# A third pair of tiles for rounded weights, and a fourth Strassen step in the second output part of each FFN

## The chip, the cores and the metric

The kernel runs on one core of one Trainium2 chip. The core has five engines that run their own instruction streams and meet at semaphores: TensorE (PE in the profile; its weight loads are shown as PEld), VectorE (DVE), ScalarE (ACT), GpSimd (POOL) and SyncE (SP), which here issues most transfers. The metric is the time of one execution in microseconds, the median of several runs. The kernel before takes 2433.58 us, median of three runs (2432.37 to 2433.91).

## The reference

One layer of an encoder on 256 positions of width 2048, in float32. With LN for a layer norm and alpha = 2^(1/4):

```
h = LN(alpha*h + 0.5*FFN1(h))
h = LN(alpha*h + (sig(gA)*(A(h) WoA) + sig(gB)*(B(h) WoB)) W_out)   # two attentions, gated
h = LN(alpha*h + CrossAttn(h, LN(mem)))                              # 4 heads, 256 memory tokens
h = LN(alpha*h + 0.5*FFN2(h))
FFN(x): g, u = split(x @ w_in);  return (silu(g) * u) @ w_out        # w_in 2048 x 11008, w_out 5504 x 2048
```

Nearly all of the work is products of 256 rows of activations with weights that are read once each from memory.

## The kernel before

**Three products for one.** A float32 value is kept as two rounded parts, `hi` (the value cast to the type fp32r) and `lo` (what the cast left over, cast too). A product is then hi·hi + hi·lo + lo·hi, three matmuls, which `mm_pair` (L300 on) and `mm_sums` (L345 on) issue with the loops `for wi in range(2)` and `for xi in range(2 - wi)`. ACT casts a weight tile to `hi` in pieces of 1024 columns (L262), and DVE subtracts to get `lo` (L265); both lines are in `halves`.

**A step.** Weights come in tiles of 128 x 2048 (1 MB): two k-tiles of 128 rows by 1024 columns. Activations are the stationary side in blocks of 128 x 128, weights move 512 columns at a time. A plain step (`mm_pair`, matmuls at L309) has 2 k-tiles x 2 row halves x 2 column halves x 3 = 24 matmuls. They add into four PSUM banks, one for each row half and column half. The last step of an odd number of k-tiles has one k-tile and 12 matmuls.

**A Strassen step** (`mm_sums`, matmuls at L363) treats the same 2 x 2 x 2 blocks with seven products in place of eight, 7 x 3 = 21 matmuls. Three of the products go into three of the group's own banks, four into four further banks that all Strassen steps of the group share. For this DVE forms sums of the weights' blocks (`weight_sums`, L246 and L248: one addition of 128 x 1024 and two of 128 x 512), which are rounded into the tiles X2 and X3 (one set of them only), and sums of the activations' blocks (`sum_forms`, L319 and L323, rounded at L253 and L254). The raw tile's own part that is rounded is then 1536 columns wide and not 2048. After the last Strassen step of a group `shared` (L674 to L679) combines the four shared banks: ACT copies two of them, DVE makes four additions.

**Where the steps lie.** An FFN is computed in two parts of 24 and 19 k-tiles of its hidden width (`F_SPLIT`). For each part, groups of 512 hidden columns are computed from x (eight steps each, Strassen steps at 2, 4 and 6), multiplied, sent through a transposing transfer and split again (`hidden`), and then the part's output is added into `h`: 2048 columns in two halves of 1024. In the first part both halves run through `out_pair`, twelve steps with Strassen steps 3, 5, 7 and 9. In the second part the first half runs through `out_pair`, ten steps with Strassen steps 3, 5 and 7, the last step with one k-tile; the second half runs through `out_proj` (matmuls at L296) in order of its blocks, without Strassen steps. `SUMS_OUT` lists which step is a Strassen step, and in which tile its activations' forms live:

```
SUMS_OUT = ({3: ("X1", 0), 5: ("X1", 1), 7: ("X0", 0), 9: ("X0", 1)},
            {3: ("X1", 0), 5: ("X1", 1), 7: ("X0", 0)})
```

Forms in X1 are made during the hidden groups; those in X0 are woven into the output part, ahead of its item 4 + 2k for the slot k (`ffn`, the loop over `homes`). The last hidden group's turn, which its own part's steps 8 and 9 read, is woven in ahead of item 6. In `pair_group` the function `then` (the shared products are added to `h`, L626 or L628) comes behind the last Strassen step, and `finish` (the four own banks are added to `h`, L747 or L749, and a norm's statistics taken) behind the last step.

**What sets the order.** `run` walks a list of items (a function, with the weights that it needs) and emits the loading and rounding of weights ahead of the item that uses them:

```
return (nxt < need + 5 and (early(queue[nxt]) or n < 2)
        and held + live + slots(queue[nxt]) <= UNITS)
```

UNITS is 2, so at most two rounded units are emitted and not yet used, beside some that have homes elsewhere. The rounded tiles come from the pools `whi` and `wlo`, with UNITS buffers each, and the raw tiles from `wraw` with three; the transfer into a raw tile is issued by SP (L191). [...] 

**Short tiles.** The pool tag `w1` (128 x 256, 1 KB of a partition) holds running totals (`total`, L283 and L284) and the activations' forms that have no home; a set of forms takes four of them. [...]

Of the kernel before, what the change touches and what calls it, by code (L numbers as in the profile page):

```python
# [27 lines left out]
SUMS_IN = {2: ("X0", 0), 4: ("X0", 1), 6: None}  # L28
AT_FIRST = 4, 6
SUMS_OUT = ({3: ("X1", 0), 5: ("X1", 1), 7: ("X0", 0), 9: ("X0", 1)},  # L30
            {3: ("X1", 0), 5: ("X1", 1), 7: ("X0", 0)})
SUMS_YB = {4: ("T0", 0), 6: ("T0", 1), 2: None}
AT_YB = (2, 4, 6), (4, 6)
SUMS_XQ = {4: ("H5", 0), 6: ("H5", 1), 2: None}
# [5 lines left out]
SUM_HOME = ("X2", "X3"),  # L40
# [10 lines left out]
UNITS = 2  # L51
# [22 lines left out]
class Act:  # L74


    def __init__(self, blocks):
        self.blocks = blocks
# [21 lines left out]
class Kernel:  # L100
    def __init__(self, ctx, tc, t, out):
        self.tc, self.nc, self.t, self.out = tc, tc.nc, t, out

        def pool(name, bufs=1, **kw):
            return ctx.enter_context(tc.tile_pool(name=name, bufs=bufs, **kw))

        self.const = pool("const")
        self.wraw = pool("wraw", 3)
        self.whi = pool("whi", UNITS)
        self.wlo = pool("wlo", UNITS)  # L110
        self.blocks = pool("blocks")
        self.res = pool("res")
        self.work = pool("work", 4)
        self.small = pool("small", 4)
        self.ps_mm = pool("ps_mm", 4, space=PSUM)
        self.ps_at = pool("ps_at", 4, space=PSUM)
        self.items = []
        self.uid = 0
        self.chain = self.sent = self.last_hi = self.ln_act = None
        self.cut = self.early = False  # L120
# [13 lines left out]
        return self.work.tile(list(shape), dt, tag="w2", bufs=6, name=self.name("w2"))  # L134

    def w1(self, shape=(P, S), dt=F32):
        return self.work.tile(list(shape), dt, tag="w1", bufs=6, name=self.name("w1"))

    def sm(self, tag, n, dt=F32, bufs=None):
        return self.small.tile([P, n], dt, tag=tag, name=self.name(tag), **({"bufs": bufs} if bufs else {}))  # L140
# [410 lines left out]
    def ffn(self, tag, xT, st, first=None, steps=None, late=None, before=None, tags=None):  # L551


        t = self.t
        f0 = bank = 0
        turn = None
        fx = {}
        for half, nf in enumerate(F_SPLIT):
            hid, fh, homes = Act([]), {}, SUMS_OUT[half]
            end = half == len(F_SPLIT) - 1  # L560
            form = lambda c, fh=fh, homes=homes, hid=hid: self.forms_step(fh, homes, c, lambda: hid)
            for g in range(-(-nf // 4)):
                j, n = f0 // 4 + g, min(4, nf - 4 * g)
                qs, ps = {}, {}
                if j == 2 and first is not None:
                    self.add(self.load_rest)
                if j == 0 and first is not None:
                    main, (ps, qs, fx) = [], first
                    self.add(lambda qs=qs: self.shared(qs, 512), prio=SOON)
                elif j == 0 and before:  # L570
                    main = self.collect(self.first_group, tag, xT, before, ps, fx)
                else:
                    src = t[tag + "_w_in"][j] if n == 4 else t[tag + "_w_in_r"][0]
                    main = self.collect(self.pair_group, bank, src, n * P, KT, xT, SUMS_IN, fx, ps, qs, None, SUM_HOME + ("H5",))
                if turn and n < 4:
                    turn[5] = turn.pop(6)
                self.weave(main, turn or {}, prio=0)
                for c, (home, _) in homes.items():
                    if home == "X1" and c // 2 == g - 1:
                        self.add(form(c))  # L580
                hidden, turn = self.hidden(ps, bank, g, n, hid, qs)
                self.add(hidden, prio=SOON)
                if before and 2 <= j < 6:
                    self.add(lambda q=j - 2: self.gb_apply(2, self.h, (q,)), prio=LATE)
                if j == 0 and first is not None:
                    for c in set(SUMS_IN) - set(AT_FIRST):
                        self.add(self.forms_step(fx, SUMS_IN, c, xT, False))
                bank ^= 1
            if end and late:
                self.add(lambda: setattr(self, "cut", True))  # L590

            def out(hid=hid):
                x = lambda: hid
                src = [t[tag + "_w_out"][g, :, f0 * 1024:(f0 + nf) * 1024] for g in range(2)]
                self.out_pair(bank, src[0], 0, nf, x, homes, fh, half == 0, st if end else None,
                              SUM_HOME + ("H5",) if end else SUM_HOME)
                if end:
                    self.out_proj(tag + "_w_out_r", nf, x, False, st, steps, tags, 2, cut=tags is None)
                else:
                    self.out_pair(bank ^ 1, src[1], 1, nf, x, homes, fh, half == 0, None)  # L600
            main = self.collect(out)

            side = dict(turn)
            if end and late:
                side[len(main) - 6] = [late]
            for c, (home, k) in homes.items():
                if home == "X0":
                    side[4 + 2 * k] = side.get(4 + 2 * k, []) + [form(c)]
            if not end:
                for i in range(2):  # L610
                    side[len(main) - 3 + i] = [self.forms_step(fx, SUMS_IN, tuple(SUMS_IN)[i], xT)]
            self.weave(main, side, prio=0)
            turn = None
            f0 += nf

    def out_pair(self, bank, src, g, nk, x, at, fx, scale, st, sums_in=SUM_HOME):

        nc, h = self.nc, self.h
        ps, qs = {}, {}

        def shared():
            for (tt, a), s in qs["add"].items():
                c = (2 * g + a) * 512
                hs = h[tt][:, c:c + 512]
                if scale:
                    nc.vector.scalar_tensor_tensor(hs, hs, ALPHA, s, ALU.mult, ALU.add)  # L626
                else:
                    nc.vector.tensor_tensor(hs, hs, s, ALU.add)  # L628

        def finish():  # L630
            for tt in range(2):
                for a in range(2):
                    self.finish(tt, 2 * g + a, ps[tt, a], scale and not at, st)
        self.pair_group(bank, src, 512, nk, x, at, fx, ps, qs, shared, sums_in)
        self.add(finish)

    def group_tile(self, j):
# [2 lines left out]
    def group_tiles(self, j):  # L640
        return {(tt, g): self.group_tile(j) for tt in range(2) for g in range(2)}

    def pair_group(self, bank, src, n, nk, x, at, fx, ps, qs, then=None, sums_in=SUM_HOME):


        steps = -(-nk // 2)
        sums = [c for c in range(steps) if c in at]
        for c in range(steps):
            kts = range(2 * c, min(2 * c + 2, nk))
            ap = src[:, kts[0] * 2 * n:(kts[-1] + 1) * 2 * n]  # L650
            if c in at:
                def fn(w, c=c):
                    if c == sums[0]:
                        qs.update((a, self.group_tile(bank + 1)) for a in range(4))
                    self.mm_sums(ps, qs, w, n, x(), fx[c], 2 * c, c == sums[0], c == sums[-1])
                self.add(fn, Sums(ap, *sums_in))
                if c == sums[-1]:
                    self.add(lambda: self.shared(qs, n), prio=SOON)
                    if then:
                        self.add(then)  # L660
                continue

            def fn(w, c=c, kts=kts):
                if c == 0:
                    ps.update(self.group_tiles(bank))
                self.mm_pair(ps, w, n, x(), kts, c == 0, c == steps - 1)
            self.add(fn, ap)

    def shared(self, qs, n):
# [1101 lines left out]
```

## Time and profile before

| what | value |
|---|---|
| median of three runs | 2433.58 us (2432.37 to 2433.91) |
| the profiled execution, span from first to last instruction | 2432.9 us |
| what the median has over that span | 0.7 us |
| PE busy | 2423.0 us, 11286 matmuls |
| DVE busy | 2121.1 us, 2423 instructions |
| ACT busy | 1551.3 us, 2017 instructions |
| transfers | 516.20 MB, 212 GB/s on average |
| granted clock of PE | 1.000 |

The profile tells of the profiled execution only its span, so the span stands for its time. Busy time counts an engine's instructions; matmuls are pipelined, so a matmul's own duration is longer than its distance from the next. The list of waits gives for each engine and line whom it waited for, the time in total, the number of waits and the longest. The chain of waits follows the work that ended last, in order of time, as start, duration and what ran. A timeline row has start, duration, engine, line, operation, output and inputs, and in brackets the idle time before it and what ended that.

### The profile page before, as it was taken

Reading aid. Unit: us, or ns where it says so; the run is one execution under the profiler, and the core shown is the slowest. Engines: PE = TensorE matmul, PEld = TensorE weight load, DVE = VectorE, ACT = ScalarE, POOL = GpSimd, SP = SyncE. Lnnn points to the kernel's source line nnn. Section 1 sums busy time; section 2 is a strip of 40 time slices with the busy share of each in tenths; the row PEclk is TensorE's granted clock in tenths of the full one; section 3 lists DMA queues with packets and bytes.
Section 4 is the critical chain, followed back from the end, with each engine's and each line's share of the span. In section 5 each row is a group of like instructions: output and inputs, shape, how many; then the busy total and the mean of one; then the engine's idle time right before and its main releaser. Section 6 shows DMA issues by size and latency. Waiting matters only on the chain.

```text
span 2432.9 us, 29701 instructions
## 1 busy us (share of the span) xinstructions
PE 2423.0 (100%) x11286; PEld 2022.5 (83%) x11286; DVE 2121.1 (87%) x2423; ACT 1551.3 (64%) x2017; POOL 36.1 (1%) x81
## 2 busy tenths in 40 slices
PE   9999999999999999999999999999999999999999
PEld 8888888889888888888888888888888888888887
DVE  8999989899878898789788889979879999888997
ACT  6676745666555557878565687765666675556762
POOL 0000000000000001000000000000000000000000
PEclk9999999999999999999999999999999999999999
DMA  7766656666645657776577577655556666666665
GB/s 268 252 214 213 208 199 221 212 199 222 225 172 209 208 209 248 230 209 175 184 249 251 167 236 218 219 184 189 190 199 214 229 221 210 216 208 205 201 223 182
DMA packets 176414, 516.20 MB, mean 212 GB/s; under 512 B 111728, under 2 KB 112496, under 8 KB 121104
## 3 DMA queue, kind: packets, MB, share of 16 engines
q1 hardware_dynamic: 170816, 495.83, 61.2%
q0 software_dynamic: 4592, 17.30, 2.2%
q8 instruction: 88, 1.44, 0.2%
q10 hardware_dynamic: 864, 1.18, 0.1%
q14 instruction: 54, 0.44, 0.1%
HBM read 485.30 MB, written 2.10 MB: 200 GB/s over the span
## 4 chain that ended last, share of the span: by engine, by line
PE 90%; DVE 4%; ACT 3%; DMA 1%; issue 1%; SPq 0%; DVEq 0%; ACTq 0%
PE at L309 24%; PE mm L309 23%; PE mm L296 11%; PE at L363 10%; PE mm L363 10%; PE mm L275 5%; PE mm L277 2%; DVE lo L265 2%; ACT hi L262 1%; PE at L1028 1%; DMA raw<-w_xq 0%; PE at L1499 0%; PE at L1082 0%; PE at L275 0%; DMA raw<-w_o_b 0%
## 5 line engine op out<-in xcount | busy, mean ns | idle before, releaser
L262 ACT CAST hi<-raw 128x1024 fp32r<-128x1024 f32 (+1 forms) x852 | 805.3, 982 | 454.2 <-PE at L309 155.0
L265 DVE TENSOR_TENSOR lo<-raw,hi 128x2048 fp32r<-128x2048 f32 (+1 forms) x427 | 902.3, 2114 | 139.3 <-ACT hi L262 133.4
L309 PE MATMUL mm<-hi,T 128*128 128x512 f32 (+1 forms) x1328 | 311.1, 384 | 1.3 <-DVE v L397 1.3
L309 PEld LDWEIGHTS mm<-hi,T 128*128 128x128 f32 x1328 | 247.3, 188 | 48.5 <-DVE v L397 1.8
L309 PE MATMUL at<-hi,T 128*128 128x512 f32 x1152 | 275.5, 389 | 0.0
L262 ACT CAST X<-H 128x1024 fp32r<-128x1024 f32 (+1 forms) x166 | 170.6, 1034 | 162.0 <-DVE H L246 128.1
L309 PEld LDWEIGHTS at<-hi,T 128*128 128x128 f32 x1152 | 216.2, 188 | 45.1
L265 DVE TENSOR_TENSOR X<-H,X 128x2048 fp32r<-128x2048 f32 (+1 forms) x83 | 186.7, 2250 | 68.6 <-ACT X L262 68.6
L309 PE MATMUL mm<-lo,T 128*128 128x512 f32 (+1 forms) x664 | 160.4, 382 | 0.0
L309 PEld LDWEIGHTS mm<-lo,T 128*128 128x128 f32 x664 | 123.7, 188 | 22.8
L309 PE MATMUL at<-lo,T 128*128 128x512 f32 x576 | 142.4, 389 | 0.0
L309 PE MATMUL at<-hi,H 128*128 128x512 f32 x560 | 133.7, 389 | 0.0
L309 PEld LDWEIGHTS at<-lo,T 128*128 128x128 f32 x576 | 108.1, 188 | 22.5
L309 PEld LDWEIGHTS at<-hi,H 128*128 128x128 f32 x560 | 104.9, 188 | 21.6
L309 PE MATMUL mm<-hi,H 128*128 128x512 f32 x480 | 115.5, 391 | 0.3 <-DVE w L679 0.3
L248 DVE TENSOR_TENSOR H<-H,raw 128x512 f32<-128x512 f32 (+1 forms) x166 | 112.2, 676 | 2.2
L309 PEld LDWEIGHTS mm<-hi,H 128*128 128x128 f32 x480 | 89.5, 188 | 19.3 <-DVE w L679 0.8
L246 DVE TENSOR_TENSOR H<-raw 128x1024 f32<-128x1024 f32 (+1 forms) x83 | 99.4, 1198 | 0.9 <-DMA raw<-w_gate 0.8
L363 PE MATMUL mm<-X,X 128*128 128x512 f32 x342 | 91.1, 392 | 0.0
L262 ACT CAST X<-raw 128x1024 fp32r<-128x1024 f32 (+1 forms) x54 | 55.4, 1036 | 48.7 <-DVE raw L248 38.7
L363 PE MATMUL at<-X,X 128*128 128x512 f32 (+1 forms) x315 | 82.5, 386 | 0.9 <-DVE X L265 0.5
L849 ACT COPY w<-w 128x1024 uint16<-128x1024 uint16 (+1 forms) x60 | 75.8, 1276 | 0.6 <-DMA w<-w 0.5
(373 smaller groups left out, 4123.1 us busy)
## 6 DMA issues: line engine op xcount, KB each, us to landing
raw<-ffn_w_in SPq DMA_DIRECT2D x150, 1024.0 KB, 4.8
raw<-ffn_w_out SPq DMA_DIRECT2D x66, 1024.0 KB, 4.8
raw<-w_gate SPq DMA_DIRECT2D x32, 1024.0 KB, 4.8
raw<-ffn_w_out_r SPq DMA_DIRECT2D x16, 1024.0 KB, 4.9
raw<-w_qk SPq DMA_DIRECT2D x16, 1024.0 KB, 5.5
raw<-w_o_b SPq DMA_DIRECT2D x16, 1024.0 KB, 4.8
raw<-w_out SPq DMA_DIRECT2D x16, 1024.0 KB, 5.2
raw<-w_xk SPq DMA_DIRECT2D x16, 1024.0 KB, 5.3
```

Of the source, the lines that this page charges most:

```text
L246: self.nc.vector.tensor_tensor(two[0], two[1], raw[:, :m].unsqueeze(1).to_broadcast([P, 2, m]), ALU.add)
L248: self.nc.vector.tensor_tensor(t[:, a * m:a * m + m], t[:, b * m:b * m + m], raw[:, a * m:a * m + m], ALU.add)
L262: self.last_hi = self.nc.scalar.copy(hi[:, c:d], src[:, c:d])
L265: self.last_lo = self.nc.vector.tensor_tensor(lo[:, :n], src, hi[:, :n].bitcast(F32), ALU.subtract)
L275: self.nc.tensor.matmul(ps, hi[j], x.both(kt), start=(j == 0), stop=False)
L277: self.last_mm = self.nc.tensor.matmul(ps[:, :S], lo[j], x.at(0, kt), start=False, stop=(j == n - 1))
L296: self.last_mm = self.nc.tensor.matmul(ps, x.at(xi, kt)[:, tt * P:(tt + 1) * P], w[wi][:, j * 512 + c:j * 512 + c + m], start=(start and j ...
L309: self.last_mm = self.nc.tensor.matmul(ps[tt, g][:, :n], x.at(xi, kt)[:, tt * P:(tt + 1) * P], w[wi][:, c:c + n], start=first and j + wi + ...
L363: self.last_mm = self.nc.tensor.matmul(bank[:, :m], a[xi], v[wi][:, c * m:(c + 1) * m], start=own and first and wi + xi == 0, stop=own and ...
L849: self.nc.scalar.copy(self.words(u, n).rearrange("p (c k) -> p k c", k=2), self.words(s, n).rearrange("p (k c) -> p k c", k=2))
L1028: nc.tensor.matmul(ps[:, c0:c0 + nk], q[:, tt * P:(tt + 1) * P], k[:, :nk], start=(j == 0), stop=(j == len(parts) - 1))
```

## The change

`whi` and `wlo` get UNITS + 1 = 3 buffers each; UNITS, and with it the order in which loads are emitted, stays 2. That takes 16 KB more of each partition. The tag `w1` gets five buffers in place of six, and the scratch for GpSimd's descriptors is set to 1024 bytes, where the library's default stood before. In the second output part of each FFN step 1 of the first half becomes a Strassen step, its forms in the second slot of X0, and the steps run in the order 0, 2, 3, 4, 5, 6, 7, 8, 1, 9. `out_pair` and `pair_group` take that order as an argument; first and last step, which open and close the sums in PSUM, go by the place in the order.

```diff
 SUMS_OUT = ({3: ("X1", 0), 5: ("X1", 1), 7: ("X0", 0), 9: ("X0", 1)},
-            {3: ("X1", 0), 5: ("X1", 1), 7: ("X0", 0)})
+            {3: ("X1", 0), 5: ("X1", 1), 7: ("X0", 0), 1: ("X0", 1)})
+ORDER_END = (0, 2, 3, 4, 5, 6, 7, 8, 1, 9)
...
-        self.whi = pool("whi", UNITS)
-        self.wlo = pool("wlo", UNITS)
+        self.whi = pool("whi", UNITS + 1)
+        self.wlo = pool("wlo", UNITS + 1)
...
-        return self.work.tile(list(shape), dt, tag="w1", bufs=6, name=self.name("w1"))
+        return self.work.tile(list(shape), dt, tag="w1", bufs=5, name=self.name("w1"))
...
-                              SUM_HOME + ("H5",) if end else SUM_HOME)
+                              SUM_HOME + ("H5",) if end else SUM_HOME, ORDER_END if end else None)
...
-        steps = -(-nk // 2)
-        sums = [c for c in range(steps) if c in at]
-        for c in range(steps):
+        order = range(-(-nk // 2)) if order is None else order
+        sums = [c for c in order if c in at]
+        for i, c in enumerate(order):
...
-            def fn(w, c=c, kts=kts):
-                if c == 0:
+            def fn(w, i=i, kts=kts):
+                if i == 0:
                     ps.update(self.group_tiles(bank))
-                self.mm_pair(ps, w, n, x(), kts, c == 0, c == steps - 1)
+                self.mm_pair(ps, w, n, x(), kts, i == 0, i == len(order) - 1)
...
-    nc = bacc.Bacc("TRN2", target_bir_lowering=False, num_devices=1)
+    nc = bacc.Bacc("TRN2", target_bir_lowering=False, num_devices=1, dynamic_dma_scratch_size=1024)
```

The arrangement of `w_out` in memory follows from `SUMS_OUT` by itself: the host swaps the two column halves of a Strassen step's k-tiles, now for step 1 too.

More of the change, by code (lines that the diff above doesn't have):

```diff
@@ L614, in ffn, with out_pair @@
             f0 += nf
-    def out_pair(self, bank, src, g, nk, x, at, fx, scale, st, sums_in=SUM_HOME):
+    def out_pair(self, bank, src, g, nk, x, at, fx, scale, st, sums_in=SUM_HOME, order=None):
         nc, h = self.nc, self.h
@@ L633, in finish @@
                     self.finish(tt, 2 * g + a, ps[tt, a], scale and not at, st)
-        self.pair_group(bank, src, 512, nk, x, at, fx, ps, qs, shared, sums_in)
+        self.pair_group(bank, src, 512, nk, x, at, fx, ps, qs, shared, sums_in, order)
         self.add(finish)
@@ L641, in group_tiles, with pair_group @@
         return {(tt, g): self.group_tile(j) for tt in range(2) for g in range(2)}
-    def pair_group(self, bank, src, n, nk, x, at, fx, ps, qs, then=None, sums_in=SUM_HOME):
-        steps = -(-nk // 2)
-        sums = [c for c in range(steps) if c in at]
-        for c in range(steps):
+    def pair_group(self, bank, src, n, nk, x, at, fx, ps, qs, then=None, sums_in=SUM_HOME, order=None):
+        order = range(-(-nk // 2)) if order is None else order
+        sums = [c for c in order if c in at]
+        for i, c in enumerate(order):
             kts = range(2 * c, min(2 * c + 2, nk))
```

## The prediction

> **What bounds the kernel now.** I read the page's engine shares first, then TensorE's waits, then the chain of waits around one part of the change, then how busy VectorE is there.
>
> ```profile
> span 2432.9 us, 29701 instructions
> PE 2423.0 (100%) x11286; PEld 2022.5 (83%) x11286; DVE 2121.1 (87%) x2423; ACT 1551.3 (64%) x2017; POOL 36.1 (1%) x81
> ```
>
> TensorE (PE) works nearly the whole span, VectorE (DVE) 87% of it. What PE waits for is short enough to be listed whole:
>
> ```profile
> PE mm L309 <- DVE v L397: 1.3, 1, 1.3
> PE at L490 <- DVE w L467: 1.1, 1, 1.1
> PE at L418 <- issue: 0.7, 1, 0.7
> PE at L363 <- DVE X L265: 0.5, 1, 0.5
> PE at L363 <- ACT X L262: 0.4, 2, 0.2
> PE mm L363 <- DVE T L254: 0.4, 1, 0.4
> PE mm L309 <- DVE w L679: 0.3, 1, 0.3
> PE at L1082 <- ACT H L849: 0.2, 1, 0.2
> PE mm L275 <- ACT hi L262: 0.2, 1, 0.2
> ```
>
> Sum 5.1 us, of which 1.1 (L490) is the start, which the change doesn't touch; 4.0 us is all the waiting that it could take away. Only 0.2 us of that is named on a weight's rounding `hi`. So the time is matmuls in a row, and less time comes from fewer matmuls. The chain of waits over the second output part of the first FFN shows what one costs:
>
> ```profile
> 580.48 16.36 PE at L309 x72
> 596.84 0.91 PE at L363 x4
> ...
> 601.37 0.23 PE at L363
> 601.60 5.44 PE at L309 x24
> ...
> 617.24 0.91 PE at L363 x4
> ...
> 622.00 8.16 PE at L309 x36
> 630.16 49.64 PE mm L296 x219
> ```
>
> Steps 0 to 2 are 72 matmuls in 16.36 us, 0.227 us each. A plain step of two k-tiles is 24 of them (5.44 us); a Strassen step (L363) takes from 596.84 to 601.60, 4.76 us, which is 21. Steps 8 and 9, after the third Strassen step, are the 36 from 622.00; at 630.16 the second half of the columns begins.
>
> **Part 1, the fourth Strassen pair.** In each FFN step 1 becomes a Strassen step and moves between steps 8 and 9. PE loses 24 − 21 = 3 matmuls, 3 × 0.227 = 0.68 us; two FFNs, −1.36 us. [...]
>
> What DVE does for one Strassen step, from its timeline in the same place:
>
> ```profile
> 593.77 0.68 DVE L319 TENSOR_TENSOR w<-H 128x512 f32<-128x512 f32 x1
> ...
> 594.98 0.48 DVE L323 TENSOR_TENSOR w<-w 128x128 f32<-128x128 f32 x2
> 595.38 0.61 DVE L323 TENSOR_TENSOR w<-w,w 128x128 f32<-128x128 f32 x2
> ...
> 604.96 0.68 DVE L254 TENSOR_TENSOR X<-w,X 128x512 fp32r<-128x512 f32 x1
> ...
> 611.78 1.22 DVE L246 TENSOR_TENSOR H<-raw 128x1024 f32<-128x1024 f32 x1
> 612.91 1.75 DVE L265 TENSOR_TENSOR lo<-raw,hi 128x1536 fp32r<-128x1536 f32 x1
> 614.58 0.68 DVE L248 TENSOR_TENSOR H<-H,raw 128x512 f32<-128x512 f32 x1
> ...
> 617.50 2.29 DVE L265 TENSOR_TENSOR X<-H,X 128x2048 fp32r<-128x2048 f32 x1 [0.70 <-ACT X L262]
> 619.71 2.29 DVE L265 TENSOR_TENSOR lo<-raw,hi 128x2048 fp32r<-128x2048 f32 x1
> ...
> 622.51 1.22 DVE L265 TENSOR_TENSOR lo<-raw,hi 128x1024 fp32r<-128x1024 f32 x1
> ...
> 626.04 1.89 DVE L628 TENSOR_TENSOR h<-h,w 128x512 f32<-128x512 f32 x3
> ```
>
> Added: the weights' sums, 1.22 + 2 × 0.68 = 2.58; the low half of those sums (L265, `X`), 2.29; the activations' forms, 0.68 + 0.48 + 0.61 + 0.68 = 2.45. Saved: 1536 columns rounded in place of 2048, 2.29 − 1.75 = 0.54. Net 2.58 + 2.29 + 2.45 − 0.54 = +6.8 us of DVE in each FFN. ScalarE (ACT) gets two more casts of the sums and one of the forms, less half a cast: by the mean of 1034 ns,
>
> ```profile
> L262 ACT CAST X<-H 128x1024 fp32r<-128x1024 f32 (+1 forms) x166 | 170.6, 1034 | 162.0 <-DVE H L246 128.1
> ```
>
> 2 × 1.03 + 0.5 − 0.5 = about 2.1 us. No transfer is added: the same 1 MB of weights is loaded, as another kind of step. Does it fit? The stretches:
>
> ```profile
> 500.00:530.00 30.00, 30.00 (x134) 24.82 (x133) 29.42 (x33) 21.65 (x27) 0.00 (x0) 1.00 0.72 211
> 580.00:630.00 50.00, 50.00 (x223) 41.42 (x221) 46.41 (x49) 30.91 (x37) 0.00 (x0) 1.00 0.65 225
> 630.00:650.00 20.00, 20.00 (x90) 16.57 (x89) 13.44 (x13) 7.51 (x9) 0.00 (x0) 1.00 0.60 200
> 251.00:303.00 52.00, 52.00 (x232) 43.04 (x230) 50.31 (x53) 36.05 (x43) 0.00 (x0) 1.00 0.61 198
> 2321.00:2371.00 50.00, 50.00 (x223) 41.50 (x222) 46.41 (x49) 30.59 (x37) 0.00 (x0) 1.00 0.66 227
> ```
>
> (Columns: stretch, its length, busy time of PE, PEld, DVE, ACT, POOL, clock, DMA share, GB/s.) The part takes 50 us with DVE busy 46.41 of it, alike in both FFNs. It becomes 49.3 us with 46.41 + 6.8 = 53.2 us of DVE work: 3.9 too much if nothing can wait. ACT, 30.91 + 2.1 of 49.3, is no bound. But after the rounding for step 8 (done at 622.0) PE needs only the 1.22 us of step 9 before 630; the other 6.8 us of those 8.0 (combining the shared products, adding them to `h`, the first rounding of the next half) can slip past 630, where DVE is busy only 13.44 of 20 us. What PE needs by the end of the new Strassen step, at 630.16 − 0.68 − 2.72 = 626.8 (step 9 is 12 matmuls), is then 53.2 − 6.8 − 1.2 = 45.2 us of work in 46.8 us, 97%. DVE ran at 98% from 500 to 530, and at 97% from 251 to 303 where Strassen and plain steps alternate in the same way, and PE lost nothing in either. I take the added wait as 0, by that nearest row; the bounds are 0 and 3.9 us in each FFN. A gain below 0 is excluded, since PE does not wait in these stretches now.
>
> Three shifts of order go with it. Step 3 comes one plain step earlier, after two and not three; that is also the order in the input groups (Strassen steps 2, 4 and 6), which fill 500 to 530. The turning of the last hidden group, woven in at the seventh item, stands one plain step nearer to step 8, which reads it; PE has one Strassen step (4.76 us) between, and its DVE work is two short subtractions. And the four banks of shared products are read out with only step 9 (2.72 us) before the next half wants two of them; those two need ACT copies alone, and ACT is a third idle here. All three are costed at nothing; if the cover is gone, what is late is PE, by the parts of a us that its waits above show (up to 1.3), and this lies inside the 3.9.
>
> **Part 2, the third pair.** Loading is still limited by UNITS = 2, so a rounding stands where it stood in each engine's order; only its wait for a free tile ends one unit earlier. These are the waits of ACT that it shortens, the three largest groups:
>
> ```profile
> ACT hi L262 <- PE at L309: 155.0, 77, 5.0
> ACT hi L262 <- PE mm L309: 119.8, 68, 5.4
> ACT hi L262 <- PE mm L296: 42.3, 13, 4.3
> ```
>
> 317 us of ACT's idle time, none of it PE's: what ends later is that PE is in work while ACT waits. The roundings behind them come up to 5.4 us sooner, and the raw tiles come free sooner for the next loads. In PE's list only the 0.2 us at L275 names `hi`; I take a gain of 0, with 4.0 us (the whole list without the start) as the most. On the other side, this pool changes when the planner believes each rounding ready, everywhere, and the planner picks each engine's order from that; bulk roundings of 2.29 us may land ahead of a short chain that PE waits for. The row nearest is the 1.3 us at L397 (such a chain in a layer norm). One more of that size at each of the five changes of stage (FFN to mixer, attention to its output, to cross attention, out of it, and into the last norm) is 6.5 us, the other bound.
>
> **Part 3, what pays for it.** Five short tiles `w1` in place of six: forms without a home hold four of them, so one is left for running totals, but these live in other stages. PE's list names no wait on a total (L283, L284); 0, at most another 0.2 us like L1082's. The scratch for GpSimd's transfers is set to 1024 bytes, where it was left at its default. Should that make an issue wait for the one before it to land, the price is this landing time:
>
> ```profile
> w<-gb POOLq DMA_DIRECT2D x24, 256.0 KB, 4.2
> ```
>
> Four stand close together once, so 3 × 4.2 = 12.6 us late at worst, for a multiply by the norm's gain; behind that in DVE's order stand roundings, and behind those PE. POOL is busy 1% of the span, and the pairs elsewhere stand apart, so I take 0. [...]
>
> **The sum.** −1.36 + 0 + 0 + 0. The profiled execution's span is 2432.9 us; the three runs have a median of 2433.58, so 0.7 us lies around the span. 2433.58 − 1.36 = **2432.2 us**.
>
> **The rivals.** *DVE becomes the bound* (the slower side). The sum of the weights for step 1 and its forms come on top of the turn and the plain rounding for step 8, and X2 and X3 exist once, so the third pair cannot start them early. If nothing slips past 630, PE waits 3.9 us in each FFN: 2433.58 − 1.36 + 7.8 = 2440.0. It decides once DVE's lateness passes 0.68 us in each FFN, and shows as slower from (4.9 + 1.36)/2 = 3.1. Against it: the two stretches at 97 and 98%. For it: here DVE already stands waiting for casts in between (0.70 at 617.50). *The third pair clears PE's waits*: 2433.58 − 1.36 − 4.0 = 2428.2. Against it: eight of nine rows name something else than a weight's rounding. *The planner's new order costs*: 2433.58 − 1.36 + 6.5 = 2438.7; for it, that every stage is planned anew, against it, that roundings done sooner are out of the way later. *Nothing happens, because PE was not the bound*: 2433.6. [...] The even 0.227 us per matmul across every quoted piece speaks against it.
>
> **How the numbers follow.** Forecast 0.60 (2430.5 to 2434.5, with up to 1.1 us of late DVE in each FFN, or half of PE's waits gone); DVE late 0.18; new order costs 0.11; waits cleared 0.06; nothing 0.05. About 0.2% (4.9 us) is what a measurement of this kernel can tell from no change, so faster begins at 2428.7 and slower at 2438.4. The gain of part 1 alone is far inside. Faster needs nearly all of the waits cleared: 0.06. Slower needs the far half of the two bad rivals: 0.13. The range leaves out these far ends: 2428.8 to 2438.2.
>
> **What would show it.** Right: 11280 matmuls; between the first out step and the next half, 49.3 us in both FFNs; no wait of PE over 1 us on `X` or `lo` at L363 there; ACT's waits for PE at `hi` cut from 317 us to a small part; POOL's loads land as before. Wrong: PE waits on DVE `X` in the new step (DVE the bound), new waits over 1 us at L418, L1028 or L275 (new order), or PE's list shrunk to under 2 us (waits cleared).

## The result and the profile after

The changed kernel takes 2463.43 us (median of four executions, 2463.03 to 2465.23) against 2433.43 beside it: ratio 1.0124, interval 1.011 to 1.0139. It is **slower by 30 us**. The forecast was 2432.2, and the range ended at 2438.2. One execution of one kernel below, the one with DVE and ACT chained, took 5366 us, for a reason not known; its other nine lie from 2428.87 to 2431.46.

The page of the changed kernel:

```profile
span 2461.8 us, 29644 instructions
PE 2429.0 (99%) x11280; PEld 2025.5 (82%) x11280; DVE 2132.7 (87%) x2443; ACT 1550.1 (63%) x2023; POOL 36.1 (1%) x81
```

The six matmuls are gone, DVE has 20 instructions and 11.6 us more, and yet the span is 28.9 us longer. With the 1.36 us of matmuls saved, 30.3 us are to be found. The first rows of its list of PE's waits (engine, line and whom it waited for: total us, times, longest):

```profile
PE mm L276 <- DVE w L285: 7.7, 2, 7.3
PE mm L310 <- DVE w L680: 6.7, 7, 2.9
PE at L364 <- ACT X L263: 3.8, 5, 1.2
PE at L310 <- DVE w L680: 2.5, 3, 1.1
PE mm L310 <- DVE w L285: 1.8, 1, 1.8
```

All twelve rows of that list sum to 28.1 us, 27.0 without the 1.1 of the start, where before had 4.0: 23.0 of the 30.3. (Line numbers after are one higher from L31 on: L680 is L679 of before.) L680 is the last step of the combination of the shared products, L285 the sum of two halves of a bank; both read PSUM, and PE waits at L276 and L310 for the bank that they free (7.3 and 2.9 us at the longest). Two such waits, in the timeline of the changed kernel (start, us, engine, line, operation, and in brackets the idle time before and what ended it):

```profile
1056.41 2.29 DVE L266 TENSOR_TENSOR lo<-raw,hi 128x2048 fp32r<-128x2048 f32 x1 [1.50 <-ACT hi L263]
1058.62 1.01 DVE L1056 SCALAR_TENSOR_TENSOR w<-at,X 128x384 f32<-128x384 f32 x2
...
1060.66 0.41 DVE L285 TENSOR_TENSOR w<-w,mm 128x256 f32<-128x256 f32 x1
...
1061.12 2.07 PE L276 MATMUL mm<-X,hi 128*128 128x512 f32 x4 [7.31 <-DVE w L285]
...
1518.20 0.69 DVE L678 TENSOR_TENSOR w<-w,w 128x512 f32<-128x512 f32 x1
1518.93 2.29 DVE L266 TENSOR_TENSOR lo<-raw,hi 128x2048 fp32r<-128x2048 f32 x1
...
1521.14 0.68 DVE L679 TENSOR_TENSOR w<-w,mm 128x512 f32<-128x512 f32 x1
1521.74 0.68 DVE L680 TENSOR_TENSOR w<-w,mm 128x512 f32<-128x512 f32 x1
...
1522.47 2.08 PE L310 MATMUL mm<-hi,H 128*128 128x512 f32 x4 [2.94 <-DVE w L680]
```

In the first, a bulk rounding of 2.29 us, which itself waited for its cast on ACT, stands ahead of the total of 1060.66, with 2.0 us of softmax work (from L1056 on) between them. In the issue order of the third pair alone, which has this same wait, the rounding and its two casts are the only instructions of DVE and ACT that stand ahead of this total and stood behind it in the kernel before; the softmax work stood ahead of it there too. In the second, a bulk rounding of 2.29 us stands between L678 and L679, in the middle of a chain for which PE waits. The second place in the kernel before:

```profile
1503.81 0.69 DVE L677 TENSOR_TENSOR w<-w,w 128x512 f32<-128x512 f32 x1
1504.53 0.69 DVE L678 TENSOR_TENSOR w<-w,mm 128x512 f32<-128x512 f32 x1
1505.14 0.68 DVE L679 TENSOR_TENSOR w<-w,mm 128x512 f32<-128x512 f32 x1
...
1505.87 1.42 PE L309 MATMUL mm<-hi,H 128*128 128x512 f32 x5 [0.33 <-DVE w L679]
```

There the chain runs in a row, and PE waits 0.33 us. Three of the longer waits in the changed kernel are followed by matmuls at a lower granted clock. Its stretches (length, busy time of PE, PEld, DVE, ACT, POOL, granted clock, DMA share, GB/s):

```profile
1061.00:1065.00 4.00, 3.88 (x11) 3.30 (x12) 2.72 (x12) 4.00 (x12) 0.00 (x0) 0.50 0.06 14
1519.00:1526.00 7.00, 4.06 (x12) 2.92 (x11) 7.00 (x9) 4.51 (x6) 0.00 (x0) 0.76 0.11 21
1619.00:1626.00 7.00, 5.17 (x17) 3.90 (x16) 5.15 (x7) 3.36 (x7) 0.00 (x0) 0.76 0.78 313
```

A clock of 0.50 over 4.0 us, and twice 0.76 over 7.0 us, where the trace has 0.50 for 3.41 us and 1.00 around it: (1 − 0.76) × 2 × 7 = 3.4 us. That is 10.8 us in which the matmuls of 512 columns start 0.427 us apart, where 0.227 is usual: by estimate 10.8 × (1 − 0.227/0.427) = 5.1 us lost. With 23.0 that makes 28.1 of 30.3; the rest lies in delays too short for the list. Matched by the number of the matmul, the kernel is 7.2 us behind at 636 us (the first FFN), 6.9 at 1050, 16.9 at 1094 (attention), 13.7 at 1468, 24.2 at 1718 (cross attention), 24.4 at 2215 and 30.3 at 2439 (the second FFN). The loss comes in four places, and most of it not where the fourth Strassen step was put.

The waits of ACT for PE at `hi`, which the prediction wanted cut to a small part, are still there, and two groups that wait for transfers have grown, from 3.7 us (`ffn_w_in`) and 14.1 us (`ffn_w_out`) before:

```profile
ACT hi L263 <- PE at L310: 108.9, 56, 3.8
ACT hi L263 <- DMA raw<-ffn_w_in: 92.2, 37, 4.8
ACT hi L263 <- PE mm L310: 83.5, 37, 3.7
ACT hi L263 <- DMA raw<-ffn_w_out: 44.2, 26, 4.2
```

### The profile page after: what moved, and what is told of

It reads as the page before. It is cut to its first block, busy times and chain, and to the rows that moved or that the text cites. A ratio compares the mean times of both kernels' runs of the same rounds, so it can differ in the third digit from the quotient of the medians.

```text
span 2461.8 us, 29644 instructions
## 1 busy us (share of the span) xinstructions
PE 2429.0 (99%) x11280; PEld 2025.5 (82%) x11280; DVE 2132.7 (87%) x2443; ACT 1550.1 (63%) x2023; POOL 36.1 (1%) x81
## 4 chain that ended last, share of the span: by engine, by line
PE 71%; DVE 11%; ACT 8%; DMA 5%; issue 4%; SPq 0%; DVEq 0%; ACTq 0%
PE mm L310 19%; PE at L310 19%; PE mm L297 9%; PE mm L364 8%; PE at L364 8%; DVE lo L266 4%; ACT hi L263 3%; PE mm L276 3%; DMA raw<-ffn_w_in 2%; PE mm L278 2%; PE at L1029 1%; ACT w L850 1%; ACT X L263 1%; DVE H L247 1%; DMA raw<-w_xv 1%
## 5 line engine op out<-in xcount | busy, mean ns | idle before, releaser
L263 ACT CAST hi<-raw 128x1024 fp32r<-128x1024 f32 (+1 forms) x852 | 802.9, 981 | 535.0 <-PE at L310 108.9
L310 PE MATMUL mm<-hi,T 128*128 128x512 f32 (+1 forms) x1328 | 310.7, 384 | 4.0 <-DVE w L680 3.5
L310 PEld LDWEIGHTS mm<-hi,T 128*128 128x128 f32 x1328 | 247.2, 188 | 52.6 <-DVE w L680 5.6
L310 PE MATMUL at<-hi,T 128*128 128x512 f32 x1152 | 275.2, 390 | 1.4 <-DVE w L680 1.4
L310 PEld LDWEIGHTS at<-hi,T 128*128 128x128 f32 x1152 | 215.8, 188 | 47.8 <-DVE w L680 3.1
L310 PE MATMUL mm<-lo,T 128*128 128x512 f32 (+1 forms) x664 | 159.7, 382 | 0.0
L310 PE MATMUL at<-lo,T 128*128 128x512 f32 x576 | 142.6, 389 | 0.0
L310 PEld LDWEIGHTS mm<-lo,T 128*128 128x128 f32 x664 | 123.6, 188 | 22.8
L310 PE MATMUL at<-hi,H 128*128 128x512 f32 x528 | 126.9, 390 | 1.1 <-DVE w L680 1.1
L310 PEld LDWEIGHTS at<-lo,T 128*128 128x128 f32 x576 | 108.1, 188 | 22.5
L310 PE MATMUL mm<-hi,H 128*128 128x512 f32 x480 | 118.8, 399 | 5.0 <-DVE w L680 3.2
L310 PEld LDWEIGHTS at<-hi,H 128*128 128x128 f32 x528 | 98.8, 188 | 22.2 <-DVE w L680 1.5
L310 PEld LDWEIGHTS mm<-hi,H 128*128 128x128 f32 x480 | 91.5, 192 | 25.6 <-DVE w L680 4.5
L364 PEld LDWEIGHTS mm<-X,X 128*128 128x128 f32 x360 | 67.0, 188 | 16.9 <-ACT X L263 1.8
```

Source lines behind the costliest of these rows:

```text
L263: self.last_hi = self.nc.scalar.copy(hi[:, c:d], src[:, c:d])
L310: self.last_mm = self.nc.tensor.matmul(ps[tt, g][:, :n], x.at(xi, kt)[:, tt * P:(tt + 1) * P], w[wi][:, c:c + n], start=first and j + wi + ...
L364: self.last_mm = self.nc.tensor.matmul(bank[:, :m], a[xi], v[wi][:, c * m:(c + 1) * m], start=own and first and wi + xi == 0, stop=own and ...
```

## The experiments

The kernel before, timed beside them, had a median of 2433.2, 2433.16 and 2433.32 us in the three groups of runs.

### The two parts alone

The third pair with what pays for it, and no fourth step:

```diff
-        self.whi = pool("whi", UNITS)
-        self.wlo = pool("wlo", UNITS)
+        self.whi = pool("whi", UNITS + 1)
+        self.wlo = pool("wlo", UNITS + 1)
...
-        return self.work.tile(list(shape), dt, tag="w1", bufs=6, name=self.name("w1"))
+        return self.work.tile(list(shape), dt, tag="w1", bufs=5, name=self.name("w1"))
...
-    nc = bacc.Bacc("TRN2", target_bir_lowering=False, num_devices=1)
+    nc = bacc.Bacc("TRN2", target_bir_lowering=False, num_devices=1, dynamic_dma_scratch_size=1024)
```

> The kernel before with the third pair of tiles, five short tiles and the small scratch, without the fourth Strassen step. Theory P (the third pair lets the planner pick another order, in which bulk roundings stand ahead of short chains that free PSUM banks): 2455 to 2466 us, most of the 30 us. Rival D (the fourth Strassen step overloads DVE at the end of both FFNs): 2432 to 2435. Rival W (five short tiles or the small scratch make the waits): 2455 to 2466 too, told from P by the run with those two alone.

Measured: 2464.51 us, ratio 1.0128 (1.0113 to 1.0143). The whole loss is here, with the same two rows first in PE's list (7.7 us at L275 for L284, 6.4 at L309 for L679).

The fourth step alone, with two pairs, six `w1` and the default scratch:

```diff
-            {3: ("X1", 0), 5: ("X1", 1), 7: ("X0", 0)})
+            {3: ("X1", 0), 5: ("X1", 1), 7: ("X0", 0), 1: ("X0", 1)})
+ORDER_END = (0, 2, 3, 4, 5, 6, 7, 8, 1, 9)
...
-        for c in range(steps):
+        for i, c in enumerate(order):
```

> The kernel before with the fourth Strassen step alone: two pairs of tiles, six short tiles, the default scratch. P: 2431 to 2435 us (six matmuls less, 1.36 us, and up to 1.3 us of late DVE in each FFN). D: 2450 us or more, with waits of PE on X or lo at the Strassen line near the end of the FFNs. W: 2431 to 2435.

Measured: 2434.79 us, ratio 1.0008 (0.9998 to 1.0018): no change that can be told. Its chain of waits over the part shows where the saving went (start, us, what ran):

```profile
580.49 10.92 PE at L310 x48
...
610.33 2.01 ACT hi L263 x2
612.34 1.02 ACT X L263
613.36 1.89 ACT w L850 x2
...
617.03 1.43 PE mm L364 x5
...
630.47 9.75 PE mm L297 x43
```

The part takes 630.47 − 580.49 = 49.98 us, where before took 630.16 − 580.48 = 49.68 and 0.68 less were foreseen. From 610.33 on, the chain runs through ACT's queue: two roundings of plain weights, the cast of a sum `X` behind them, copies, and then the matmul. With two pairs the new step makes ACT late, not DVE.

What pays for the third pair, alone:

```diff
-        return self.work.tile(list(shape), dt, tag="w1", bufs=6, name=self.name("w1"))
+        return self.work.tile(list(shape), dt, tag="w1", bufs=5, name=self.name("w1"))
...
-    nc = bacc.Bacc("TRN2", target_bir_lowering=False, num_devices=1)
+    nc = bacc.Bacc("TRN2", target_bir_lowering=False, num_devices=1, dynamic_dma_scratch_size=1024)
```

> The kernel before with five short tiles and the small scratch alone. P and D: 2432 to 2435 us. W: 2440 us or more, with the wait of 7 us on a total in the attention stretch, or late GpSimd loads.

Measured: 2433.74 us, ratio 1.0003 (0.9993 to 1.0012). It costs nothing that can be measured.

### The tiles or the order

A third pair does two things: it lets a rounding start one unit earlier, and it lets the planner, the step of the framework that writes each engine's issue order, write out another order for every engine. The issue orders of the two programs, compared instruction by instruction, differ in 1581 of 2422 places on DVE, 1341 of 1942 on ACT and 836 of 11107 on PE; on DVE 990 instructions now stand behind a rounding that they stood ahead of. The five short tiles and the small scratch have no part in this: with those alone, DVE, PE and SP keep the order of the kernel before, and ACT's differs in 3 places. The next kernel has the tiles of the first experiment, and at the end of planning every engine's instructions are chained in the order that the kernel before has. The chain's edges are of the class `NoSync`.

```diff
+def pin(tc):
+    """Queue each engine's instructions in the order of ORDER."""
...
+            if prev is not None:
+                tc.add_manual_dep(i, prev.name, info, reason="pin")
+            prev = i
...
     Kernel(ctx, tc, t, out).build()
+    pin(tc)
```

> As e1 (third pair, five short tiles, small scratch), but every engine's instructions are queued in exactly the order that they have in the kernel before, by issue-order edges between neighbours; the third pair then only ends waits for a free tile sooner. P: 2429 to 2434 us. If the tiles themselves cost (where they lie, transfers that start sooner), or W: 2445 us or more. D: 2432 to 2435.

Measured: 2427.39 us, **ratio 0.9975 (0.9964 to 0.9986)**: faster than both kernels, 37.1 us faster than the same tiles in the planner's order, and below the 2429 to 2434 that were expected. Its list of PE's waits is short again:

```profile
PE mm L309 <- DVE v L397: 1.3, 1, 1.3
PE at L490 <- DVE w L467: 1.1, 1, 1.1
PE mm L309 <- DVE w L679: 0.4, 1, 0.4
PE mm L363 <- DVE T L254: 0.3, 1, 0.3
PE at L418 <- DVE h L410: 0.3, 1, 0.3
```

So the tiles gain and the order loses. The list of before names too little for that gain: its rows sum to 5.1 us and these to 3.4, yet the span fell from 2432.9 to 2425.6. Most of the gain lies in delays so short that the profile counts them as PE at work. Measured from each matmul's start to the next one's, against the usual distance of that kind of matmul (the 30th percentile in the trace of before), the delays ahead of the Strassen step's matmuls whose moving side is a sum `X` come to 5.0 us in the trace of before and 0.9 here. That is 4.1 of the 7.1 us by which all such delays together are less (a kind being one line, one set of tiles and one shape; with kinds cut otherwise both figures move by some tenths). The groups of before show it faintly (busy, mean ns | idle before):

```profile
L363 PE MATMUL mm<-X,X 128*128 128x512 f32 x342 | 91.1, 392 | 0.0
L363 PE MATMUL at<-X,X 128*128 128x512 f32 (+1 forms) x315 | 82.5, 386 | 0.9 <-DVE X L265 0.5 <-ACT X L262 0.4
```

and the same groups with the third pair in before's order:

```profile
L363 PE MATMUL mm<-X,X 128*128 128x512 f32 x342 | 90.2, 389 | 0.0
L363 PE MATMUL at<-X,X 128*128 128x512 f32 (+1 forms) x315 | 81.5, 383 | 0.0
```

One case, in the timeline of before:

```profile
562.83 1.57 ACT L262 CAST hi<-raw 128x1024 fp32r<-128x1024 f32 x2 [3.17 <-PE mm L309]
...
565.54 1.04 ACT L262 CAST X<-H 128x1024 fp32r<-128x1024 f32 x1
...
566.64 0.96 PE L363 MATMUL at<-X,X 128*128 128x384 f32 x4 [0.20 <-ACT X L262]
```

and with the third pair in the same order:

```profile
560.73 1.57 ACT L262 CAST hi<-raw 128x1024 fp32r<-128x1024 f32 x2 [2.96 <-DMA raw<-ffn_w_in_r]
...
563.43 1.04 ACT L262 CAST X<-H 128x1024 fp32r<-128x1024 f32 x1
...
564.92 0.85 PE L363 MATMUL at<-X,X 128*128 128x384 f32 x4
```

The plain rounding waits for its data now and no longer for PE to give a tile back; the cast of the sum behind it in ACT's queue comes 2.1 us sooner, 1.2 of which the kernel had gained by then, and PE doesn't wait for it.

The changed kernel whole, chained in the order of the program with the fourth step alone:

```diff
     Kernel(ctx, tc, t, out).build()
+    pin(tc)
```

> The changed kernel whole (third pair, fourth Strassen step, five short tiles, small scratch), with every engine's instructions queued in the order that the kernel with the fourth step alone (e2) has. If the order is all that cost: 2425 to 2428 us, the 2427.4 of e4 less 1.36. If the fourth step's late DVE, which made e2 1.6 us slower and not 1.4 faster, is not cured by the third pair: 2428 to 2431. If the fourth step needs the new order: 2440 or more.

Measured: 2428.68 us, ratio 0.9978 (0.9968 to 0.9987). The chain of waits over the part:

```profile
578.66 10.92 PE at L310 x48
...
627.66 12.47 PE mm L297 x55
```

627.66 − 578.66 = 49.00 us, 0.68 less than before; in the second FFN it is 49.17. With a third pair the fourth step brings its saving in one FFN, and most of it in the other. The whole is 1.3 us above the kernel without it, which is within what can be told, and just outside the 2425 to 2428 expected if the order were all that cost. Its second expectation, 2428 to 2431 with DVE late in the fourth step, has the number but not the place: by the starts of like matmuls in the two profiled executions, the two parts gain 0.7 and 0.5 us on the kernel without the fourth step, and some 2.5 us are lost elsewhere.

The opposite test, two pairs in the new order, wasn't run: that order starts a third rounding ahead of work that frees the first, and by the author's estimate the queue would wait for itself, which no run shows.

### Which queue, and which overtaking

The third pair, with each rounding kept from standing ahead of shared products (L674 to L679) and totals (L283, L284) emitted before it; all else as the planner likes. The edit is in `halves`, which rounds the sums `X` too, so it holds these back as well:

```diff
+    def after(self, k):
+        s = self.short[k]
+        return self.tc.issue_after(s.ins) if s is not None else nullcontext()
...
-            self.last_hi = self.nc.scalar.copy(hi[:, c:d], src[:, c:d])
+            with self.after(0):
+                self.last_hi = self.nc.scalar.copy(hi[:, c:d], src[:, c:d])
...
-        with self.tc.issue_after(self.chain.ins) if self.chain is not None else nullcontext():
+        with self.after(1), self.tc.issue_after(self.chain.ins) if self.chain is not None else nullcontext():
...
-        nc.scalar.copy(b, q[1])
+        self.short[0] = nc.scalar.copy(b, q[1])
...
-        nc.vector.tensor_tensor(c, b, q[3], ALU.subtract)
+        self.short[1] = nc.vector.tensor_tensor(c, b, q[3], ALU.subtract)
```

> As e1 (third pair without the fourth step, planner free), but the roundings of weight tiles may not be queued ahead of shared products and running totals that were emitted before them (issue order alone, on ACT and DVE). Theory O (roundings that overtake the reading out of PSUM banks make PE's waits): 2428 to 2440 us. Rival (the rest of the new order costs: casts against turns and softmax, PE's order): 2450 or more.

Measured: 2448.07 us, ratio 1.0054 (1.0038 to 1.0071): 16.4 us of the first experiment's 31 are back, between the two ranges that were expected, so neither holds as it stood. The first rows of PE's list (lines here are up to six higher; L369 is L363 of before):

```profile
PE at L369 <- ACT X L268: 4.6, 6, 1.8
PE at L369 <- DVE X L271: 3.4, 2, 2.4
PE mm L283 <- DVE lo L271: 1.9, 1, 1.9
```

The waits for L679 and L284 have left the top; what PE waits for instead are sums and roundings that stand too late. So the 16.4 us are what is left after a new cost, and don't measure what the overtakings held back here had cost.

Then the first experiment's kernel with one engine alone chained in before's order: DVE, PE, ACT, and last DVE and ACT together.

```diff
     Kernel(ctx, tc, t, out).build()
+    pin(tc)
```

> As e1, with DVE alone in the order of the kernel before; the planner orders ACT, PE and SP anew around it. If DVE's order carries the cost: 2427 to 2440 us. If ACT's does: 2450 or more.

> As e1, with PE alone in the order of the kernel before. O and every theory that blames the order of DVE or ACT: 2455 to 2466 us. If PE's own order (which step's matmuls are taken between) carries the cost: 2427 to 2440.

> As e1 (third pair, no fourth step), with ACT alone in the order of the kernel before. If the costs of DVE's and of ACT's new order add up, ACT's share is what e7 left, 2441.5 - 2427.4 = 14 us, and this run gives 2448 to 2453 us. If DVE's order follows from ACT's (a low half is queued when its cast is ready), more comes back: 2428 to 2445. If ACT's order is only a consequence of DVE's: 2460 or more.

> As e1, with DVE and ACT in the order of the kernel before, PE, SP and POOL left to the planner. If these two carry all of the cost: 2426 to 2430 us. If the order of PE or of the loads has a part of its own: 2433 or more.

| chained in before's order | median, us | ratio to before (interval) | against no chain |
|---|---|---|---|
| none | 2464.51 | 1.0128 (1.0113 to 1.0143) | |
| PE | 2468.08 | 1.0141 (1.0125 to 1.0156) | +3.6 |
| ACT | 2448.07 | 1.006 (1.0043 to 1.0076) | −16.4 |
| DVE | 2441.47 | 1.0036 (1.0024 to 1.0047) | −23.0 |
| DVE and ACT | 2429.9 | 0.9986 (0.9976 to 0.9995) | −34.6 |
| all | 2427.39 | 0.9975 (0.9964 to 0.9986) | −37.1 |

ACT's and the pair's medians lie in the ranges expected for costs that add up and for two engines that carry all; DVE's and PE's lie 1.5 and 2.1 us above the ranges that fit them. PE's own order brings nothing back: with PE alone chained, its list still begins

```profile
PE mm L309 <- DVE w L679: 8.1, 8, 2.8
```

The order on DVE and ACT is worth 34.6 of 37.1 us. The two taken singly sum to 39.4, some 5 us more than both together. A likely reason, not tested, is that they share a delay: the high half is cast on ACT and then subtracted on DVE, and a chain that PE waits for goes through both. Nor is a row one engine's share alone, since the order of the engines not chained was left to the planner each time.

## Why the prediction was wrong

**Where it failed.** In Part 2, in the sentence "a rounding stands where it stood in each engine's order; only its wait for a free tile ends one unit earlier". The reason given was that UNITS, which limits loading, stays at 2. But the order changed all the same: with the third pair alone 1581 of 2422 places of DVE's queue, two thirds, differ from before, and with the five short tiles and the small scratch alone none do. That the planner goes by the tiles that are free, beside the loads that UNITS limits, is the author's reading of this; no run shows how it decides. The same part saw a new order as a bound, "bulk roundings of 2.29 us may land ahead of a short chain that PE waits for", and the timeline at 1518.93 is exactly that. The size was the other error: one wait of 1.3 us "at each of the five changes of stage" made 6.5 us. The waits came at the shared products and totals, up to 7.3 us long, and at half clock after three of them. Against the same tiles in the old order it is 37.1 us, nearly six times the bound. The row taken as the nearest, a chain in a layer norm, was the wrong neighbour: the trace of before had a wait at L309 for L679 of 0.3 us, and what should have been asked is how long it gets with a rounding of 2.29 us in the chain.

**The planner's new order costs**, the rival at 0.11 and 2438.7, was right in kind and in direction, and too small; the sign that the prediction named for it, a new wait over 1 us at L275, came (7.3 us). The argument held against it, that "roundings done sooner are out of the way later", was not borne out: 990 instructions of DVE, which is busy 87% of the span, came to stand behind a rounding that they had stood ahead of.

**The third pair at 0**: wrong as well, in the other direction. "4.0 us (the whole list without the start) as the most" fell: in the old order it gains 5.8 us by the medians and 7.3 by the profiled spans. The list of waits was taken for all of PE's waiting, and the even 0.227 us for a sign that there was none besides; 4.1 us of what was gained stood ahead of matmuls that read sums, most of it in delays that the list folds into busy time (its own two rows for `X` hold 0.9). "Only 0.2 us of that is named on a weight's rounding `hi`" was true and misled: in the case shown the sum `X` was late because a `hi` ahead of it on ACT waited for a tile.

**Part 1**: the matmuls are 11280, the saving of 0.68 us in an FFN is there (49.00 for 49.68) once the third pair is and the order is kept, and 0.51 in the second. DVE's added work was put a little high: it measured 11.6 us in both FFNs, 5.8 in each, for the 6.8 of the sum. "DVE becomes the bound" doesn't hold: no PE wait over 1 us in the part names DVE. With two pairs ACT is late (49.98), which the prediction had ruled out by ACT's share of the stretch, 30.91 + 2.1 of 49.3; what mattered was where the roundings stood in its queue. In the changed kernel itself the part took 50.5 us in the first FFN, by the starts of its matmuls, and 50.1 in the second: there the new order eats the saving. The waits listed in them are for a sum `X`, 0.7 and 0.2 us; one of 1.2 us comes 15 us ahead of the second.

**Part 3** at 0 was right: 1.0003 (0.9993 to 1.0012).

**ACT's waits** "cut from 317 us to a small part" came true only in the old order. In the changed kernel 108.9 and 83.5 us are left in the two largest groups, of 155.0 and 119.8. In the old order the largest group of ACT's waits for PE at `hi` is

```profile
ACT hi L262 <- PE at L309: 34.2, 17, 3.4
```

**What stays open.** The order costs the 37.1 us, and DVE's and ACT's orders carry nearly all; which overtakings carry how much is shown for single waits only. Holding roundings behind shared products and totals brings 16.4 us back, net of the waits for sums that it makes, so the other 20.7 can't be put down to other overtakings. And 1.3 us between the two fastest kernels is inside what a run can tell.

## What to carry to other kernels

Where a planner writes each engine's order, the size of a pool can change that order (here a third pair moved 1581 of DVE's 2422 places and cost 31 us): before adding a buffer, compare the issue orders of the two programs, and time the buffer once with the old order kept. Keep bulk work that can wait (here roundings of 2.29 us) behind the short operations that free what the bottleneck engine needs next; here, on an engine 87% busy, the place in the queue decided and not the share. And a list of waits can name less than a busy engine waits (here 1.7 us of a gain of 7.3 was in it): compare start-to-start distances of like instructions before calling its waits exhausted.

## What the hardware showed that was not expected

Three waits of a few us cost PE more than their own length. In the changed kernel the granted clock is at 0.50 after waits of 7.31 and 2.94 us, and after one of only 1.82 us:

```profile
1621.07 3.87 PE L310 MATMUL mm<-hi,H 128*128 128x512 f32 x9 [1.82 <-DVE w L285]
```

Nine matmuls take 3.87 us, 0.43 each where 0.227 is usual; the half clock lasts 3.41 us after each of the two shorter waits.

The length of a wait doesn't decide it alone. With the third pair alone, waits of 2.81 and 2.61 us are followed by matmuls near the usual pace, six in 1.66 us and four in 1.19, and the granted clock is 1.00 for 4.0 us behind each:

```profile
1522.57 1.66 PE L309 MATMUL mm<-hi,H 128*128 128x512 f32 x6 [2.81 <-DVE w L679]
...
1621.06 1.19 PE L309 MATMUL mm<-hi,H 128*128 128x512 f32 x4 [2.61 <-DVE w L284]
```

In the changed kernel's trace the half clock of the three waits begins at 1058.28, 1522.50 and 1621.48 us and lasts 6.83, 3.41 and 3.41 us; the three starts lie 464.22 and 98.98 us apart, 136 and 29 times the 3.413 us that the trace has for each of the shorter two. Whether it counts when a wait falls, beside how long it is, no run here was made to test.
